# Zero-padded low halves, a fused BK and 14 earlier projection matmuls in the recurrent features of a hybrid block

## The chip, the cores and the metric

One NeuronCore of a Trainium2 chip runs the whole kernel. The metric is the device time of one execution in microseconds (us). A core has five instruction streams that run side by side and wait for one another through semaphores: TensorE (PE, with its weight loads shown apart as PEld), VectorE (DVE), ScalarE (ACT), GpSimd (POOL) and SyncE (SP, which here starts most DMAs). Each stream runs its own instructions in order.

## The reference, cut to what matters

One transformer-like layer on 1024 tokens of width 1024: a wide input projection, dilated window attention on part of it, an RWKV-7 recurrence on another part, a gated mix of both, and a mixture of 32 experts. The change is in the features of the recurrence:

```python
pm = pf + (prev - pf) * shift_mu                  # pf: the projection p = rms_norm(x) @ w_in
r, k, v, xw, xa, xg = split(pm)
decay = exp(-exp(-softplus(-(w0 + tanh(xw) @ w_up)) - 0.5))
a  = sigmoid(a0 + xa @ a_up)                      # w_up and a_up: 64 x 512, the "lora" weights
kk = normalize_per_head(k * k_k)
k  = k * (1 + (a - 1) * k_a)
o  = wkv7_scan(r, decay, k, v, kk, kk * a)        # state update by -kk and by kk*a
```

## The kernel before, in words

**Numbers.** A float32 product is made of three TensorE products: both operands are split into a high part (type F32R) and a low part, and high x high, high x low and low x high are summed in PSUM. For the lora products the contraction has only 64 rows. So the input tile `xw` holds the high part of tanh(xw) in rows 0 to 63 and its low part in rows 64 to 127 (`xa` the other way round), the host gives the weights twice, and one 128-row matmul with `lh` (L572) makes high x high and high x low. The third product, low weights by high input, is a matmul over 64 rows, `ll[hrs[n]]` by `t[hrs[n]]` (L573).

**Stages.** Up to about 110 us the kernel loads x and projects the first columns. From 110 to about 400 us it makes the recurrent features (`prep(p)`, p = 0 to 3, each with two halves h of 512 tokens; below they are half 0 to half 7 in the order of time). Then come the scan over chunks, the attention (to about 900 us), the mix, the routing, and the experts (from about 1180 us to the end).

**Fillers.** The projection of the remaining columns is cut into single 128x512 matmuls (L306), 48 for one column tile, and kept in a list of generators. `fill(n)` takes the next n of them; calls of `fill` stand all over `prep`, the scan and the attention, so that TensorE has work while the chain of small steps goes on. `fill` also steps the triangular solve (`tstep_`) once in 14 matmuls. What is left over is done by `need` before the next `prep`, or after the scan. The program order is not the final one: a scheduler orders the instructions of each engine by its own estimate of when their inputs are there, so a filler can land ahead of or behind the place at which it was written.

**One half of `prep`.** Four lora matmuls (L572, L573) make `pw` and `pa`. A small matmul (L578) and a chain of 12 tiny DVE steps give the norm of kk, ACT spreads it (L583), and PE transposes it (L588) beside the transposes of v (L592). DVE makes `kk` (L611), a running sum (L602) and, through ACT's exponentials, `P`, `iP` and `sg`. POOL makes half of `AR` (L618) from the tile `tc`, which DVE's L624 overwrites afterwards. Then come the other half of `AR` (L616) and the tile `BK`: its outer quarters from `kp` (L626), its middle from `kk * a * iP` (L628 to L630). `t2` (L632) is for a side result. PE transposes BK in 8 matmuls (L642), and multiplies BK by AR in 32 matmuls over 64 rows (L667). `split_w` turns each new weight tile of the projection into `wh` on ACT (L275) and `wl` on DVE (L277); `wh` has two buffers.

Of the kernel before, what the change touches and what calls it, by code (L numbers as in the profile page):

```python
# [10 lines left out]
F32 = mybir.dt.float32  # L11
F32R = mybir.dt.float32r
# [4 lines left out]
ALU = mybir.AluOpType  # L17
# [8 lines left out]
DEC = math.exp(-0.5)  # L26
FT, FS, FP, FA, FU, GL = 20, 6, 2, 9, 9, 10
FI, FQ, TP, FR, SQ, SG, SB, UJ, QW, QL, QT, QJ = 14, 2, 1, 16, 1, 0, 1, 1, 1, 0, 0, 1
LP, LB, LR, PF, MP, QB, GB, NY = 0, 0, 0, 1, 0, 1, 2, 2
DILS = (1, 4, 16)  # L30
NEG = -1e30
# [150 lines left out]
def block_kernel(ctx, tc, I, out, dbg=None):  # L182
    nc = tc.nc
# [96 lines left out]
    def pb(shape):  # L280
        return psB.tile([128] + shape, F32, name="pb")
# [38 lines left out]
    for k in range(8):  # L320
# [4 lines left out]
        if k == 7:  # L325
# [3 lines left out]
                                       op0=ALU.mult, op1=ALU.subtract)  # L329
        for i in range(2):  # L330
            for kk in ([k] if i == 0 or k > 1 else [] if k == 0 else [0, 1]):
                for h in range(2):
                    hs = slice(h * 512, (h + 1) * 512)
                    for n, (a, b) in enumerate(((0, xhi), (0, xlo), (1, xhi))):
                        nc.tensor.matmul(ps0[i][h], w0[i][a][:, kk, :], b[:, kk, hs],
                                         start=(kk == 0 and n == 0), stop=(kk == 7 and n == 2))
    for h in range(2):
        hs = slice(h * 512, (h + 1) * 512)
        for k in range(8):
            for n, (a, b) in enumerate(((0, xhi), (0, xlo), (1, xhi))):  # L340
                nc.tensor.matmul(ps0[2][h], w0[2][a][:, k, :], b[:, k, hs], start=(k == 0 and n == 0),
                                 stop=(k == 7 and n == 2))
# [22 lines left out]
    def tstep(n=1):  # L365
        for _ in range(n):
            if side and next(side[0], 1) == 1:
                side.pop(0)
# [21 lines left out]
    def fill(n):  # L390
        while n > 0 and fillers:
            try:
                next(fillers[0])
                n -= 1
                filled[0] += 1
                if filled[0] % FI == 0:
                    tstep()
            except StopIteration:
                fillers.pop(0)
# [11 lines left out]
    hrs = [slice(0, 64), slice(64, 128)]  # L411
# [32 lines left out]
    p1 = s1.enter_context(tc.tile_pool(name="p1a", bufs=1, reuse_waits="tile"))  # L444
# [33 lines left out]
    for p in range(4):  # L478
        cs = slice(128 * p, 128 * p + 128)
        for h in range(2):  # L480
            hs = slice(h * 512, (h + 1) * 512)
            ps = pb([512])
# [28 lines left out]
    p1 = s1.enter_context(tc.tile_pool(name="p1", bufs=1, reuse_waits="tile"))  # L511
# [2 lines left out]
    Bm = p1.tile([128, 4, 2, 2, 64], F32, name="Bm")  # L514
    nc.gpsimd.memset(Bm, 0.0)

    rkv = {}

    def rkv_steps(p):
# [24 lines left out]
    def prep(p):  # L544
# [6 lines left out]
        lr = p1.tile([128, 2, 128], F32, name="lr")  # L551
        nc.sync.dma_start(lr, I["lora"][p])
        lh = p1.tile([128, 2, 128], F32R, name="lh")
        nc.scalar.activation(lh, lr, AF.Copy)
        ll = p1.tile([128, 128], F32R, name="ll")
        for n, hr in enumerate(hrs):
            nc.vector.tensor_tensor(ll[hr], lr[hr, n], lh[hr, n].bitcast(F32), op=ALU.subtract)

        def tstep():
            if TP:  # L560
                tstep_()
            fill(FP)
        for h in range(2):
            hs = slice(h * 512, (h + 1) * 512)
            j0 = 4 * h

            def T(tag):
                return p1.tile([128, 512], F32, tag=tag, name=tag)

            pw, pa = pb([512]), pb([512])  # L570
            for n, (ps, t) in enumerate(((pw, xw), (pa, xa))):
                nc.tensor.matmul(ps, lh[:, n], t[:, hs], start=True, stop=False)  # L572
                nc.tensor.matmul(ps, ll[hrs[n]], t[hrs[n], hs], start=False, stop=True)  # L573
            kks = T("ta")
            nc.scalar.activation(kks, k[:, hs], AF.Square, scale=pc("kk", p))
            pn = pb([8])
            for j in range(4):
                nc.tensor.matmul(pn[:, 2 * j:2 * j + 2], kks[:, j * 128:(j + 1) * 128], cc("ind2"),  # L578
                                 start=True, stop=True)
# [11 lines left out]
            for j in range(4):  # L591
# [6 lines left out]
            at = T("at")  # L598
# [6 lines left out]
            iP = T("iP")  # L605
# [4 lines left out]
            kk = T("kk")  # L610
            nc.vector.scalar_tensor_tensor(kk, k[:, hs], pc("kk", p), pr.rearrange("q a b -> q (a b)"),  # L611
                                           op0=ALU.mult, op1=ALU.mult)
            AR = p1.tile([128, 4, 256], F32, name="AR")
            BK = p1.tile([128, 4, 256], F32, name="BK")
            c4 = lambda ap: ap.rearrange("q (c t) -> q c t", t=128)
# [3 lines left out]
                                    op=ALU.mult)  # L619
# [5 lines left out]
            for c in range(2):  # L625
                nc.vector.tensor_tensor(BK[:, :, 192 * c:192 * c + 64], c4(kp)[:, :, 64 * c:64 * c + 64],  # L626
                                        c4(iP)[:, :, 64 * c:64 * c + 64], op=ALU.mult)
            nc.vector.tensor_scalar(at, at, 0.5, 0.5, op0=ALU.mult, op1=ALU.add)  # L628
            nc.gpsimd.tensor_tensor(kk, kk, at, op=ALU.mult)
            nc.vector.tensor_tensor(BK[:, :, 64:192], c4(kk), c4(iP), op=ALU.mult)  # L630
            t2 = T("ta")
            nc.vector.scalar_tensor_tensor(t2, r[:, hs], pc("rk", p), kp, op0=ALU.mult, op1=ALU.mult)  # L632
            stq.dma_start(dAR[j0:j0 + 4, :, p].rearrange("j q m -> q j m"), AR)
            tstep()

            BT = p1.tile([128, 4, 2, 128], F32, name="BT")
            for jj in range(2):
# [23 lines left out]
            for hh in range(2):  # L661
                hr = hrs[hh]
# [87 lines left out]
    for p in range(4):  # L750
        prep(p)
        if p % 2 == 1:
            side.append(solve(p // 2))
# [56 lines left out]
    for j in range(8):  # L810
# [17 lines left out]
        for c in range(2):  # L828
# [4 lines left out]
            for hh in range(2):  # L833
                hr = hrs[hh]
                pX.append(pb([4, 64]))
                for p in range(4):
                    nc.tensor.matmul(pX[hh][ra, p], AR[hr, p, 64:128] if c == 0 else AR[hr, p, 128:192], Z[hr, p],
                                     start=(p == 0), stop=True, skip_group_check=True)
# [18 lines left out]
            for hh in range(2):  # L857
                hr = hrs[hh]
                for p in range(4):
                    nc.tensor.matmul(pX[hh][ro, p], AR[hr, p, 0:64] if c == 0 else AR[hr, p, 192:256], Z[hr, p],  # L860
                                     start=(p == 0), stop=False, skip_group_check=True)
# [302 lines left out]
    for n in range(8):  # L1164
        wh, wl = wrs.pop(n)
        for h in range(2):
            hs = slice(512 * h, 512 * h + 512)
            ga = gate(1, n, h)
            ps = psA.tile([128, 512], F32, name="pa")
# [31 lines left out]
    for tag in ("ohi", "olo"):  # L1201
        t = pf.tile([128, 8, 512], F32, tag=tag, name=tag + "g")
        gas += [t[:, j] for j in range(8)]
    for h in range(2):
        hs = slice(512 * h, 512 * h + 512)
        for n in range(8):
# [3 lines left out]
            ps = psA.tile([128, 512], F32, name="pa")  # L1210
# [211 lines left out]
    for i in range(8):  # L1422
# [7 lines left out]
        for c in range(2):  # L1430
            cs = slice(512 * c, 512 * c + 512)
            ps = psA.tile([128, 512], F32, name="pa")
# [267 lines left out]
```

## Time and profile before

| what | us |
|---|---|
| median of 3 runs (lowest, highest) | 1754.18 (1747.92, 1766.67) |
| the profiled execution, its own time | 1749.15 |
| its span in the trace | 1747.4 |
| PE busy | 1667.3 |
| DVE busy | 1204.8 |
| ACT busy | 871.5 |
| POOL busy | 299.8 |

"Busy" is the time in which an instruction of that engine was under way; the rest of the span is idle. Matmuls overlap one another, so the pace of PE is read from the distance between starts, not from the duration of one. "PEclk" or the clock column is the share of its full clock that TensorE was granted: 1.00 or 0.50 in this trace, or a mean of the two over a stretch. A start time such as 160.12 is us from the span's start; "[2.41 <-DVE BK L630]" behind a row says that the engine was idle for 2.41 us before it and that the write of BK at line 630 by DVE ended this.

### The profile page before, as it was taken

What the parts mean: (1) busy time and instruction counts of PE and PEld (TensorE: products, weight loads), DVE (VectorE), ACT (ScalarE), POOL (GpSimd) and SP (SyncE); (2) the same over time, 40 slices, a digit from 0 to 9 for tenths busy, and PEclk for the clock granted to TensorE, in tenths of its full rate; (3) what the DMA queues carried; (4) which work ended last, traced back from release to release, by engine and by line L of the source; (5) the groups of instructions that cost most, each with busy time, mean ns of one, the idle gap of its engine ahead of it and who ended that gap; (6) DMA issues with size and microseconds to landing.
All of it is one profiled execution on the core that took longest, in us unless ns stands there. A gap on an engine that the chain in (4) does not pass through costs nothing. (4 is left out here: it accounts for less than half of the span.)

```text
span 1747.4 us, 25870 instructions
## 1 busy us (share of the span) xinstructions
PE 1667.3 (95%) x9395; PEld 1321.3 (76%) x9396; DVE 1204.8 (69%) x2181; ACT 871.5 (50%) x1315; POOL 299.8 (17%) x321
## 2 busy tenths in 40 slices
PE   8999999999999999999998899979999999999996
PEld 6677777777777777777777677758888888888884
DVE  5647798575664444344436666589999999998985
ACT  4523434332231233343344122278888888887774
POOL 0110113123432000000000131112222221221211
PEclk9998999799999999999999899979999999999998
DMA  8323333355762111111138884479999999999993
GB/s 292 138 74 125 95 107 115 110 193 180 232 205 85 37 38 42 43 50 43 52 113 272 253 291 144 182 250 372 375 380 373 371 368 368 371 364 372 360 371 114
DMA packets 145619, 363.44 MB, mean 208 GB/s; under 512 B 17316, under 2 KB 62772, under 8 KB 145484
## 3 DMA queue, kind: packets, MB, share of 16 engines
q1 hardware_dynamic: 123108, 303.67, 48.1%
q0 software_dynamic: 15872, 50.35, 10.3%
q10 hardware_dynamic: 6504, 7.69, 1.6%
q8 instruction: 76, 1.25, 0.3%
q14 instruction: 59, 0.48, 0.1%
HBM read 307.49 MB, written 62.29 MB: 212 GB/s over the span
## 5 line engine op out<-in xcount | busy, mean ns | idle before, releaser
L1529 PE MATMUL pb<-u,xTh 128*128 128x512 f32 x1024 | 338.6, 406 | 0.5 <-ACT xTh L1524 0.5
L306 PE MATMUL pa<-xlo,wh 128*128 128x512 f32 x736 | 307.6, 418 | 0.0
L306 PE MATMUL pa<-xhi,wl 128*128 128x512 f32 x736 | 302.3, 411 | 2.2 <-DVE wl L277 2.2
L306 PE MATMUL pa<-xhi,wh 128*128 128x512 f32 x736 | 301.5, 410 | 1.5 <-DVE raw L426 1.0
L1415 DVE TENSOR_TENSOR u<-raw,u 128x1024 fp32r<-128x1024 f32 x216 | 255.0, 1219 | 18.1 <-ACT u L1414 14.6
L1414 ACT ACTIVATE u<-raw 128x1024 fp32r<-128x1024 f32 x216 | 223.7, 1056 | 31.6 <-PE pb L1529 19.7
L1529 PEld LDWEIGHTS pb<-u,xTh 128*128 128x128 f32 x1024 | 191.4, 189 | 40.5 <-ACT xTh L1524 1.4
L1529 PE MATMUL pb<-u,xTl 128*128 128x512 f32 x512 | 207.7, 406 | 0.3 <-DVE xTl L1525 0.3
L306 PEld LDWEIGHTS pa<-xlo,wh 128*128 128x128 f32 x736 | 141.2, 192 | 40.7 <-issue 11.0
L306 PEld LDWEIGHTS pa<-xhi,wl 128*128 128x128 f32 x736 | 141.6, 192 | 34.4 <-issue 3.3
L306 PEld LDWEIGHTS pa<-xhi,wh 128*128 128x128 f32 x736 | 141.4, 192 | 34.4 <-issue 2.9
L1415 DVE TENSOR_TENSOR u<-mix,u 128x1024 fp32r<-128x1024 f32 x128 | 151.5, 1218 | 11.2 <-ACT u L1414 9.1
L1529 PE MATMUL pa<-u,hTh 128*128 128x512 f32 x512 | 143.4, 401 | 0.9 <-ACT hTh L1524 0.9
L1414 ACT ACTIVATE u<-mix 128x1024 fp32r<-128x1024 f32 x128 | 133.2, 1057 | 16.6 <-PE pb L1529 9.2
L977 DVE SCALAR_TENSOR_TENSOR Sb<-pb,rqk,bias 128x128 f32<-128x128 f32 (+1 forms) x96 | 35.5, 407 | 124.5 <-PE pb L976 116.6
L1508 POOL DMA_INDIRECT out<-row,tba x30 | 78.5, 2617 | 202.5 <-ACT u L1414 171.9
L1529 PEld LDWEIGHTS pb<-u,xTl 128*128 128x128 f32 x512 | 96.9, 189 | 18.5 <-DVE xTl L1525 1.0
L1529 PEld LDWEIGHTS pa<-u,hTh 128*128 128x128 f32 x512 | 93.5, 188 | 22.4 <-ACT hTh L1524 1.5
L275 ACT ACTIVATE wh<-wr 128x1024 fp32r<-128x1024 f32 x49 | 51.8, 1056 | 113.5 <-PE pa L306 95.1
L1529 PE MATMUL pa<-u,hTl 128*128 128x512 f32 x256 | 80.7, 396 | 1.2 <-DVE hTl L1525 1.2
L1502 POOL DMA_INDIRECT xin<-dH,tbl x32 | 38.5, 1203 | 250.7 <-PE pb L1523 247.5
L981 ACT ACTIVATE Sb<-Sb,ML 128x128 f32<-128x128 f32 (+1 forms) x96 | 42.3, 442 | 54.7 <-DVE ML L979 54.7
(415 smaller groups left out, 2872.8 us busy)
## 6 DMA issues: line engine op xcount, KB each, us to landing
raw<-in_w_expert_up SPq DMA_DIRECT2D x72, 512.0 KB, 11.7
raw<-in_w_expert_gate SPq DMA_DIRECT2D x71, 512.0 KB, 4.9
raw<-in_w_expert_down SPq DMA_DIRECT2D x71, 512.0 KB, 11.8
wr<-in_w_in SPq DMA_DIRECT2D x49, 512.0 KB, 3.5
mix<-in_w_expert_down SPq DMA_DIRECT2D x46, 512.0 KB, 13.5
mix<-in_w_expert_gate SPq DMA_DIRECT2D x42, 512.0 KB, 5.0
mix<-in_w_expert_up SPq DMA_DIRECT2D x40, 512.0 KB, 11.8
dGA<-gs POOLq DMA_DIRECT2D x32, 256.0 KB, 3.3
```

The lines of the kernel that those rows point to most:

```text
L275: nc.scalar.activation(wh, wr, AF.Copy)
L306: nc.tensor.matmul(ps, a[:, k, :], b[:, k, hs], start=(n == 0), stop=(n == 23))
L977: nc.vector.scalar_tensor_tensor(Sb[:, hh, 0:nk], pS[:, 0:nk], u.rn[:, 0, i, hh:hh + 1], u.bias[:, hh, 256 - nk:], op0=ALU.mult, op1=ALU.add)
L981: nc.scalar.activation(Sb[:, hh, 0:nk], Sb[:, hh, 0:nk], AF.Exp, bias=u.ML[:, i, hh:hh + 1], accum_out=u.ML[:, i, 2 + hh:3 + hh])
L1414: nc.scalar.activation(hi, raw, AF.Copy)
L1415: nc.vector.tensor_tensor(lo, raw, hi.bitcast(F32), op=ALU.subtract)
L1502: nc.gpsimd.indirect_dma_start(out=dst, out_offset=None, in_=src, in_offset=bass.IndirectOffsetOnAxis(ap=idx, axis=0), bounds_check=S - 1, ...
L1508: nc.gpsimd.indirect_dma_start(out=out, out_offset=bass.IndirectOffsetOnAxis(ap=idx, axis=0), in_=src, in_offset=None, compute_op=ALU.add)
L1529: nc.tensor.matmul(ps, x, w, start=first, stop=last)
```

## The change

Three edits in `prep`, and a constant `FB = 14`:

```diff
+    ll = p1.tile([128, 2, 128], F32R, name="ll")
+    nc.gpsimd.memset(ll.bitcast(F32), 0.0)
...
-        ll = p1.tile([128, 128], F32R, name="ll")
         for n, hr in enumerate(hrs):
-            nc.vector.tensor_tensor(ll[hr], lr[hr, n], lh[hr, n].bitcast(F32), op=ALU.subtract)
+            nc.vector.tensor_tensor(ll[hr, n], lr[hr, n], lh[hr, n].bitcast(F32), op=ALU.subtract)
...
-                nc.tensor.matmul(ps, ll[hrs[n]], t[hrs[n], hs], start=False, stop=True)
+                nc.tensor.matmul(ps, ll[:, n], t[:, hs], start=False, stop=True)
...
-            nc.vector.tensor_scalar(at, at, 0.5, 0.5, op0=ALU.mult, op1=ALU.add)
-            nc.gpsimd.tensor_tensor(kk, kk, at, op=ALU.mult)
-            nc.vector.tensor_tensor(BK[:, :, 64:192], c4(kk), c4(iP), op=ALU.mult)
+            nc.vector.scalar_tensor_tensor(kk, at, 1.0, kk, op0=ALU.add, op1=ALU.mult)
+            nc.vector.scalar_tensor_tensor(BK[:, :, 64:192], c4(kk), 0.5, c4(iP), op0=ALU.mult, op1=ALU.mult)
...
             tstep()
+            fill(FB)
 
             BT = p1.tile([128, 4, 2, 128], F32, name="BT")
```

First, the low part of the lora weights gets a tile of full height, set to zero once, of which each `prep` rewrites the same halves; its matmul runs over 128 rows, 64 of them zeros. Second, a = 0.5 * at + 0.5 is no longer made by a step of its own: kk becomes (at + 1) * kk on DVE, in place of a DVE step and a POOL multiplication, and the factor 0.5 goes into the product with `iP`. Third, `fill(14)` stands ahead of the transposes of BK, in each of the 8 halves. The number of fillers in the program (2208 matmuls of L306) stays the same.

Where the scheduler puts things shows in the order of the built programs. On TensorE, at the transposes of BK in half 1 (`ident` is the identity, `sg` and `at` hold the split t2; line numbers of the change are 1 to 3 higher than before). Before:

```order
L306 MATMUL pa<-xhi,wh 128x512
L306 MATMUL pa<-xlo,wh 128x512
L642 MATMUL pb<-ident,BK 128x128 x8
L306 MATMUL pa<-xhi,wl 128x512
L652 MATMUL pb<-sg,onr 128x512
L667 MATMUL pb<-AR,BK 128x128 x7
L653 MATMUL pb<-at,onr 128x512
L667 MATMUL pb<-AR,BK 128x128 x9
```

and of the change:

```order
L307 MATMUL pa<-xhi,wh 128x512
L307 MATMUL pa<-xlo,wh 128x512
L645 MATMUL pb<-ident,BK 128x128 x8
L655 MATMUL pb<-sg,onr 128x512
L656 MATMUL pb<-at,onr 128x512
L670 MATMUL pb<-AR,BK 128x128 x16
```

The fillers that stood behind the transposes have moved ahead of them, but not 14 at each place. Counted over all halves, the fillers between the transposes of kk's norm and v (L588, L592) and those of BK were 27, 28, 35, 35, 31, 32, 36, 25, and are 28, 31, 36, 28, 27, 38, 37, 28 (half 5 has matmuls of the solve in between). Ahead of L588 they were 21, 13, 17, 13, 43, 37, 15, 16 (counted from the small matmuls L578) and are 21, 15, 17, 21, 36, 38, 12, 20.

On VectorE, the stretch from `kk` to BK in half 1, before:

```order
L611 SCALAR_TENSOR_TENSOR kk<-k,pv,pb 128x512
L622 TENSOR_SCALAR ta<-at,ka_377 128x512
L628 TENSOR_SCALAR at<-at 128x512
L600 TENSOR_SCALAR sg<-sg 128x512
L602 SCALAR_TENSOR_TENSOR tb<-cv,sg 128x512
L607 TENSOR_TENSOR sg<-tb,sg 128x512
L624 TENSOR_TENSOR tc<-k,ta 128x512
L616 TENSOR_TENSOR AR<-sg,kk 128x4x128
L626 TENSOR_TENSOR BK<-tc,iP 128x4x64 x2
L630 TENSOR_TENSOR BK<-kk,iP 128x4x128
L632 SCALAR_TENSOR_TENSOR ta<-r,pv,tc 128x512
```

and of the change:

```order
L614 SCALAR_TENSOR_TENSOR kk<-k,pv,pb 128x512
L603 TENSOR_SCALAR sg<-sg 128x512
L625 TENSOR_SCALAR ta<-at,ka_377 128x512
L605 SCALAR_TENSOR_TENSOR tb<-cv,sg 128x512
L610 TENSOR_TENSOR sg<-tb,sg 128x512
L627 TENSOR_TENSOR tc<-k,ta 128x512
L619 TENSOR_TENSOR AR<-sg,kk 128x4x128
L629 TENSOR_TENSOR BK<-tc,iP 128x4x64 x2
L631 SCALAR_TENSOR_TENSOR kk<-at,kk 128x512
L634 SCALAR_TENSOR_TENSOR ta<-r,pv,tc 128x512
L632 SCALAR_TENSOR_TENSOR BK<-kk,iP 128x4x128
```

The step on `at` (L628) is gone and the running sum stands one place earlier; the new product kk (L631) stands behind the outer quarters of BK, and t2 has come ahead of the last step of BK, which is now the last of the three.

Also on VectorE, the end of the norm's chain in half 3 (`rn`, `rsq_z`: the norm's tiny tiles; `wl`: the low part of the next weight tile). Before:

```order
L262 TENSOR_TENSOR rsq_z<-rn 128x8
L263 TENSOR_TENSOR rsq_z<-rsq_z,rsq_u 128x8
L264 SCALAR_TENSOR_TENSOR rn<-rsq_z,rn 128x8
L534 TENSOR_TENSOR raw<-pa,rstdB 128x512
L611 SCALAR_TENSOR_TENSOR kk<-k,pv,pb 128x512
```

and of the change:

```order
L263 TENSOR_TENSOR rsq_z<-rn 128x8
L538 TENSOR_TENSOR raw<-pa,rstdB 128x512
L264 TENSOR_TENSOR rsq_z<-rsq_z,rsq_u 128x8
L278 TENSOR_TENSOR wl<-wr,wh 128x1024
L265 SCALAR_TENSOR_TENSOR rn<-rsq_z,rn 128x8
L540 SCALAR_TENSOR_TENSOR v<-raw,pv,v 128x512
L603 TENSOR_SCALAR sg<-sg 128x512
L614 SCALAR_TENSOR_TENSOR kk<-k,pv,pb 128x512
```

Here `wl`, and what it waits for, has come ahead of the norm's last step; half 7 has the same.

More of the change, by code (lines that the diff above doesn't have):

```diff
@@ L28 @@
 FI, FQ, TP, FR, SQ, SG, SB, UJ, QW, QL, QT, QJ = 14, 2, 1, 16, 1, 0, 1, 1, 1, 0, 0, 1
+FB = 14
 LP, LB, LR, PF, MP, QB, GB, NY = 0, 0, 0, 1, 0, 1, 2, 2
```

## The prediction

> **What bounds the kernel now.** I read the page's busy times first, then the busy time by stage, then TensorE's waits and its clock inside the stage of the change.
>
> ```profile
> PE 1667.3 (95%) x9395; PEld 1321.3 (76%) x9396; DVE 1204.8 (69%) x2181; ACT 871.5 (50%) x1315; POOL 299.8 (17%) x321
> ```
>
> TensorE is under way for 95% of the span. The rows by stage (from:to, length, then busy PE, PEld, DVE, ACT and POOL with counts, the granted clock, DMA share, GB/s) say where the other 5% is:
>
> ```profile
> 110.00:400.00 290.00, 270.09 (x1536) 213.88 (x1535) 222.83 (x522) 108.47 (x190) 51.63 (x76) 0.91 0.38 125
> 400.00:640.00 240.00, 234.85 (x2281) 184.39 (x2279) 124.74 (x314) 66.21 (x127) 63.06 (x86) 1.00 0.40 127
> 640.00:900.00 260.00, 259.24 (x1439) 189.89 (x1439) 105.96 (x224) 100.40 (x251) 12.85 (x21) 1.00 0.17 58
> ```
>
> The stage of the change is the first row. It has 20 us without a matmul and a mean clock of 0.91. The next two stages are filled by TensorE (235 of 240, 259 of 260), so what the first stage saves is handed on. The experts read their weights through DMA, but not before the mix has given its buffers back:
>
> ```profile
> 1080.00:1120.00 40.00, 39.94 (x210) 31.63 (x209) 23.43 (x118) 10.81 (x28) 8.06 (x8) 1.00 0.31 111
> 1180.00:1737.00 557.00, 551.66 (x2564) 458.21 (x2562) 513.83 (x515) 452.65 (x512) 115.09 (x60) 1.00 0.99 357
> ```
>
> DMA is at 0.31 shortly before and at 0.99 from 1180 us on. So the weight stream is not already running full when the experts begin; it starts from a point that compute sets and moves with it. The chain that ended last is of no use here: it holds only the last 1.7 us.
>
> TensorE's idle time in the first stage is mostly one wait, for BK; these are its six places in the order of time:
>
> ```profile
> PE pb L642 <- DVE BK L630: 13.2, 6, 2.6
> 160.12 1.48 PE L642 MATMUL pb<-ident,BK 128*128 128x128 f32 x8 [2.41 <-DVE BK L630]
> 195.18 1.06 PE L642 MATMUL pb<-ident,BK 128*128 128x128 f32 x8 [2.20 <-DVE BK L630]
> 223.07 1.06 PE L642 MATMUL pb<-ident,BK 128*128 128x128 f32 x8 [2.62 <-DVE BK L630]
> 255.52 1.06 PE L642 MATMUL pb<-ident,BK 128*128 128x128 f32 x8 [0.76 <-DVE BK L630]
> 326.82 1.06 PE L642 MATMUL pb<-ident,BK 128*128 128x128 f32 x8 [2.63 <-DVE BK L630]
> 361.94 1.89 PE L642 MATMUL pb<-ident,BK 128*128 128x128 f32 x8 [2.57 <-DVE BK L630]
> ```
>
> These are halves 1, 2, 3, 4, 6 and 7. The second loss stands right behind some of them (stretch, length, busy PE, clock, DMA share, GB/s):
>
> ```profile
> 160.60:174.30 13.70, 13.70 (x52) 0.50 0.30 96
> 193.00:198.00 5.00, 2.82 (x16) 1.00 0.49 161
> 220.40:227.00 6.60, 3.98 (x27) 1.00 0.34 120
> 327.90:351.80 23.90, 23.90 (x83) 0.50 0.22 77
> 362.00:365.40 3.40, 3.40 (x13) 0.50 0.00 1
> ```
>
> After the gaps of 2.41, 2.63 and 2.57 us TensorE works at half clock for 13.7, 23.9 and 3.4 us; after those of 2.20 and 2.62 us it keeps the full clock. So a gap of this size may cost the clock or not. What half clock means is the distance between fillers:
>
> ```profile
> 121.37 0.63 PE L306 MATMUL pa<-xhi,wh 128*128 128x512 f32 x1
> 121.80 0.63 PE L306 MATMUL pa<-xlo,wh 128*128 128x512 f32 x1
> 123.32 0.39 PE L306 MATMUL pa<-xhi,wl 128*128 128x512 f32 x1
> 123.55 0.40 PE L306 MATMUL pa<-xhi,wh 128*128 128x512 f32 x1
> ```
>
> 0.43 us against 0.23 (0.235 over longer runs): 45% of a half-clock stretch is lost. The three stretches together are 41.0 us, so they cost 18.4 us.
>
> **The change part by part. Low halves.** One half's four lora matmuls and the two fillers behind them, and below them the first two fillers behind the float32 transposes:
>
> ```profile
> 141.88 0.47 PE L572 MATMUL pb<-xw,lh 128*128 128x512 f32 x1
> 142.28 0.50 PE L573 MATMUL pb<-xw,ll 64*128 64x512 f32 x1
> 142.72 0.50 PE L572 MATMUL pb<-xa,lh 128*128 128x512 f32 x1
> 143.15 0.50 PE L573 MATMUL pb<-xa,ll 64*128 64x512 f32 x1
> 143.58 0.50 PE L306 MATMUL pa<-xhi,wl 128*128 128x512 f32 x1
> 143.91 0.40 PE L306 MATMUL pa<-xhi,wh 128*128 128x512 f32 x1
> 150.91 0.47 PE L306 MATMUL pa<-xlo,wh 128*128 128x512 f32 x1
> 151.22 0.40 PE L306 MATMUL pa<-xhi,wl 128*128 128x512 f32 x1
> ```
>
> The five steps from 141.88 to 143.91 take 2.03 us, at full clock. With all of them over 128 rows I expect the fillers' 0.235, except for the first, which still follows matmuls of another type and takes 0.31 as at 150.91: 0.31 + 4 x 0.235 = 1.25. That saves 0.78 a half, **6.2 us** in 8 halves, on TensorE itself. Bounds: nothing, if it is something else than the height that slows them, and 6.9 us if the first goes at 0.235 too. I take 6.2, since it is the alternation of heights that sets these rows apart from all other 128x512 rows. [...]
>
> The zeroing of `ll` is one POOL instruction for the whole stage; POOL is busy for 51.6 of 290 us there and nothing else waits behind it for long: nothing.
>
> **BK.** Half 1 on DVE and POOL:
>
> ```profile
> 150.86 0.75 DVE L611 SCALAR_TENSOR_TENSOR kk<-k,pv,pb 128x512 f32<-128x512 f32 x1 [0.80 <-PE pb L588]
> 152.90 1.22 DVE L602 TENSOR_TENSOR_SCAN tb<-cv,sg 128x512 f32<-128x512 f32 x1
> 156.34 0.69 DVE L624 TENSOR_TENSOR tc<-k,ta 128x512 f32<-128x512 f32 x1 [1.49 <-POOL AR L618]
> 157.55 1.82 DVE L626 TENSOR_TENSOR BK<-tc,iP 128x256 f32<-128x256 f32 x2
> 159.29 0.68 DVE L630 TENSOR_TENSOR BK<-kk,iP 128x512 f32<-128x512 f32 x1
> 159.90 0.74 DVE L632 SCALAR_TENSOR_TENSOR ta<-r,pv,tc 128x512 f32<-128x512 f32 x1
> 157.71 1.37 POOL L629 TENSOR_TENSOR kk<-kk,at 128x512 f32<-128x512 f32 x1 [1.41 <-DVE AR L616]
> ```
>
> POOL's product hides behind L626, and L626 pays for it: two steps of 256 columns take 1.74 us to the next start while POOL runs (I take 0.66 without it, somewhat over half of the 0.61 from L630's start to the next for each). So not 0.4 + 1.4 us go, but the step on `at` (0.33) ahead of the running sum, which also moves ahead of L622: the sum starts 1.46 instead of 2.04 us after `kk`, 0.58 earlier. POOL's L618, which waits for the sum, and L624 go with it: L624 starts at 155.76. From there 0.61 (L624), 0.61 (L616), 0.66 (L626 twice), 0.67 (new kk), 0.67 (t2, now ahead), 0.74 (new BK), and 0.15 to TensorE, which is what lies between the end at 159.97 and 160.12: BK's transposes can start at 159.87 instead of 160.12. Only 0.25 us, since t2 stands in between and the fused steps are each a little longer than what they replace. The 3 fillers more that stand ahead of the transposes fill 0.70. The gap goes from 2.41 to about **1.45 us**.
>
> The same working for the others, by the same row durations and the row orders of the change; a fused step counts 0.67, a step on `at` 0.33, and a step that POOL stretched to 1.7 us (`k`'s mixing step in half 2, t2 in halves 4 and 6, the two L626 in half 7) loses about 1.0. Half 2: `at` and the stretched step of 1.7 go from ahead of BK, two fused steps and 0.06 come, 0.65 earlier in all; one filler more: 2.20 to 1.3. Half 3: four small steps ahead of the running sum (1.8) and the stretching go, the fused steps come, 2.8 us earlier from `kk` to BK; but 7 fillers fewer (1.65; they went ahead of L588): 2.62 to 1.4, and 0.5 more at L588 (below). Half 4: 1.6 earlier, 4 fillers fewer: 0.76 to 0.1. Half 6: `at` and 1.0 go, one fused step comes, 0.65 earlier; one filler more: 2.63 to 1.8. Half 7: the sum 0.8 earlier and 1.0 less stretching, two fused steps more, 0.4 earlier; 3 fillers more: 2.57 to 1.5. Sum 8.0 instead of 13.2: **5.2 us** saved. Bounds: 0 and 13.2.
>
> **14 fillers.** They add no work; what they cost is what is missing later. The stages that lose them are the ones with 235 of 240 and 259 of 260 us busy, and the projection runs on into the attention, so it is taken from a place where TensorE had work anyway: nothing. The solve steps that `fill` calls come a little earlier; DVE carries them either way.
>
> **Clock.** Of the 18.4 us I count halves 1 and 7 (6.2 and 1.5 us) as won, since their gaps shrink to 1.5 us, and half of the 10.7 us of half 6, whose 1.8 us is uncertain: **13.0 us**. Bounds: nothing and 18.4. The smallest gap that lost the clock at once is 2.41, the largest that kept it 2.62; the half clock at 121 us above stands behind none of these gaps, so a smaller one is not safe. [...]
>
> **Sum.** 6.2 + 5.2 + 13.0 = 24.4 us, from the profiled execution's own 1749.15 to 1724.8. That execution was 5.0 us faster than the median of the three runs shown (1754.18), as is plausible where the clock falls by chance; I carry this along and forecast a median of **1730 us**.
>
> **The rivals.** *The clock stays out.* The gaps shrink, but the half-clock stretches stay or come back elsewhere, because work with few active rows (L667's 64) holds the clock down once it is down: in the stretch from 327.9 on TensorE had work all the time and stayed at 0.50 for 23.9 us. Then 6.2 + 5.2 = 11 us: 1743. For it: two of the gaps kept the clock as they were, so it is not the gap's length alone. Against it: each of the three stretches starts within 1.1 us of the end of a gap.
>
> *The chain rules.* If the stage is held by the chain through DVE (222.8 of 290 us busy) and not by TensorE, then what TensorE saves in the lora matmuls becomes more waiting for BK, and since t2 now stands ahead, BK is not earlier: nothing is won, 1754. This is also what happens if the scheduler's order undoes the 14 fillers; in halves 3 and 4 it has put fewer ahead of BK than before. Against it: the chain starts at L588, and 12 or more fillers stand ahead of that in each half, so it follows TensorE's pace.
>
> *Slower: `wl` ahead of the norm.* In halves 3 and 7 DVE must now do `wl` (L277) before the last step of the norm, and `wl` waits for ACT's `wh`, which waits for TensorE to finish a column tile:
>
> ```profile
> 209.58 0.63 ACT L583 ACTIVATE ta<-rn 128x512 f32<-128x512 f32 x1 [0.19 <-DVE rn L264]
> 210.72 1.06 ACT L275 ACTIVATE wh<-wr 128x1024 fp32r<-128x1024 f32 x1 [0.51 <-PE pa L306]
> 215.56 1.20 DVE L277 TENSOR_TENSOR wl<-wr,wh 128x1024 fp32r<-128x1024 f32 x1
> ```
>
> From the tile's last filler to L588 go 1.06 for L275, 1.20 for L277, 0.2 for the norm's tiny step, 0.63 for L583 and some 0.5 for hand-overs of 0.15 each, 3.6 us; TensorE has 13 fillers, 3.1 us. That is the 0.5 us above. If ACT has something else before it, or POOL stretches `wl` as it does L626, the gap passes 2.4 us from 2 us of delay on, and TensorE loses its clock there. Two new gaps of 2.5 us, each with a stretch like the longest one (10.7 us), are 26 us, against 11 won: 15 us slower, 1769.
>
> **How the numbers follow.** Forecast 0.47 (1715 to 1737, the low end from the upper bounds 6.9, 9 of the gaps, and 18.4), clock stays out 0.28 (1737 to 1748), chain rules 0.15 (1748 to 1760), slower 0.10. The range takes the first two and part of the third: 1716 to 1752. Faster by over 1% (below 1736.6) is the forecast and a little of the second: 0.50; within 1%: 0.40; slower: 0.10. One per cent is about what a measurement of this kernel can tell from no change; its three runs spread over 1.1%.
>
> **What would show it.** Low halves: the four lora matmuls start 0.24 us apart at full clock. BK: POOL's product is gone, two L626 steps take under 0.9 us, t2 lies directly ahead of the last BK step, and TensorE's wait at BK is near 8 us in six places instead of 13.2. Clock: over 0.95 in the stage, with no stretch at 0.50 over 10 us. The stage ends some 24 us earlier, and the later ones are as long as before. I am wrong if the gaps grow, if a wait at L588 appears, or if the clock is below 0.91 there.

## The result and the profile after

The changed kernel takes **1726.52 us** (median of 4 runs, 1724.14 to 1729.95) against 1756.53 for the kernel before beside it: ratio 0.9843, 95% interval 0.9806 to 0.988. Run once more later, it took 1727.87 us (median of 5; ratio 0.9882, 0.9837 to 0.9927). The forecast was 1730, with a range of 1716 to 1752. The profiled execution took 1724.65 us; the sum worked out from rows was 1724.8.

The page of the changed kernel, and two rows by stage (columns as before: stretch, length, busy PE, PEld, DVE, ACT, POOL, clock, DMA share, GB/s):

```profile
span 1722.9 us, 25856 instructions
PE 1646.6 (96%) x9395; PEld 1307.5 (76%) x9396; DVE 1193.8 (69%) x2181; ACT 870.6 (51%) x1315; POOL 290.7 (17%) x314
...
110.00:400.00 290.00, 273.34 (x1959) 220.60 (x1957) 228.33 (x551) 117.14 (x205) 52.90 (x86) 0.98 0.41 138
1155.00:1712.00 557.00, 552.40 (x2570) 458.85 (x2568) 513.99 (x515) 453.29 (x514) 115.18 (x60) 1.00 0.99 357
```

In the same 290 us TensorE got through 1959 matmuls instead of 1536, at a clock of 0.98 instead of 0.91, while its busy time hardly moved (273 against 270 us). Of the 423 more, 352 are small ones of the solve and the scan, which have moved into the window. The clock, more than the busy share, shows the gain. The experts' stage is the row of before moved by 25 us: 552 us busy in 557, DMA at 0.99.

In the list of TensorE's waits (us in total, times, longest) the one for BK, and below it from the timeline the six gaps ahead of BK's transposes and one at the solve:

```profile
PE pb L645 <- DVE BK L632: 7.6, 6, 1.6
```

```profile
161.45 1.06 PE L645 MATMUL pb<-ident,BK 128*128 128x128 f32 x8 [1.37 <-DVE BK L632]
188.35 1.06 PE L645 MATMUL pb<-ident,BK 128*128 128x128 f32 x8 [1.57 <-DVE BK L632]
213.52 1.06 PE L645 MATMUL pb<-ident,BK 128*128 128x128 f32 x8 [1.46 <-DVE BK L632]
240.12 1.06 PE L645 MATMUL pb<-ident,BK 128*128 128x128 f32 x8 [0.19 <-DVE BK L632]
311.30 1.06 PE L645 MATMUL pb<-ident,BK 128*128 128x128 f32 x8 [1.51 <-DVE BK L632]
335.84 1.06 PE L645 MATMUL pb<-ident,BK 128*128 128x128 f32 x8 [1.47 <-DVE BK L632]
380.46 1.20 PE L730 MATMUL pb<-YT,LW 32*32 32x32 f32 x64 [1.64 <-DVE YT L722]
```

7.6 us instead of 13.2. The row at 335.84 stands 26.1 us earlier than its counterpart at 361.94. Behind these gaps the clock holds; what is left of half clock lies ahead of half 1 and behind the solve's wait (rows by stretch):

```profile
119.20:126.00 6.80, 6.80 (x19) 5.54 (x20) 5.23 (x17) 2.76 (x6) 1.47 (x2) 0.50 0.31 96
126.00:382.00 256.00, 241.52 (x1594) 195.58 (x1594) 216.43 (x522) 104.65 (x185) 42.80 (x68) 1.00 0.43 144
382.00:385.40 3.40, 3.40 (x79) 2.55 (x79) 0.00 (x0) 0.87 (x2) 3.23 (x6) 0.50 0.51 154
```

A second profile, of the later execution at 1727.87 us, has the same 7.6 us of gaps at BK and no half clock behind them either. It has half clock at 119.2 and 382.0 us as well, but also in two places more, behind waits of 1.20 us for the next `wl` and of 1.38 us at the solve in half 5:

```profile
259.20:262.60 3.40, 3.40 (x8) 2.72 (x9) 3.40 (x12) 1.41 (x2) 0.00 (x0) 0.50 0.53 159
279.60:286.40 6.80, 6.80 (x141) 5.92 (x141) 2.88 (x4) 5.70 (x11) 3.52 (x7) 0.50 0.37 113
```

In the first profile waits of 1.20 and 1.56 us stand at these two places, and the clock held. So what a gap there does to the clock differs from one execution to the next.

From the timeline of the first profile the lora matmuls of half 1 with two fillers, and DVE's steps around the fused ones:

```profile
143.47 0.48 PE L575 MATMUL pb<-xw,lh 128*128 128x512 f32 x1
143.78 0.39 PE L576 MATMUL pb<-xw,ll 128*128 128x512 f32 x1
144.01 0.40 PE L575 MATMUL pb<-xa,lh 128*128 128x512 f32 x1
144.25 0.39 PE L576 MATMUL pb<-xa,ll 128*128 128x512 f32 x1
144.48 0.40 PE L307 MATMUL pa<-xhi,wl 128*128 128x512 f32 x1
144.72 0.40 PE L307 MATMUL pa<-xhi,wh 128*128 128x512 f32 x1
```

```profile
158.68 0.76 DVE L629 TENSOR_TENSOR BK<-tc,iP 128x256 f32<-128x256 f32 x2
159.35 0.69 DVE L631 SCALAR_TENSOR_TENSOR kk<-at,kk 128x512 f32<-128x512 f32 x1
159.95 0.75 DVE L634 SCALAR_TENSOR_TENSOR ta<-r,pv,tc 128x512 f32<-128x512 f32 x1
160.61 0.69 DVE L632 SCALAR_TENSOR_TENSOR BK<-kk,iP 128x512 f32<-128x512 f32 x1
```

Five steps from 143.47 to 144.72 are 1.25 us instead of 2.03; seven of the eight halves have 1.24 to 1.31, and half 0, which holds a wait for `ll`, has 1.63. Where the 0.2 us of each step went shows in the weight loads (PEld) of the first low half, before and after:

```profile
142.28 0.18 PEld L573 LDWEIGHTS pb<-xw,ll 64*128 64x128 f32 x1 [0.24 <-issue]
143.55 0.19 PEld L576 LDWEIGHTS pb<-xw,ll 128*128 128x128 f32 x1
```

Over 64 rows the load starts at 142.28, together with its own matmul; at full height it starts 0.23 us ahead of its matmul at 143.78, beside the matmul in front. The two L629 take 0.67 to the next start instead of 1.74, t2 (L634) stands ahead of BK's last step, and TensorE starts 0.15 us after that.

### The profile page after: what moved, and what is told of

It is laid out like the page before. It is cut to its first block, busy times and chain, and to the rows that moved or that the text cites. A ratio compares the mean times of both kernels' runs of the same rounds, so it can differ in the third digit from the quotient of the medians.

```text
span 1722.9 us, 25856 instructions
## 1 busy us (share of the span) xinstructions
PE 1646.6 (96%) x9395; PEld 1307.5 (76%) x9396; DVE 1193.8 (69%) x2181; ACT 870.6 (51%) x1315; POOL 290.7 (17%) x314
## 3 DMA queue, kind: packets, MB, share of 16 engines
q8 instruction: 76, 1.25, 0.3%
## 5 line engine op out<-in xcount | busy, mean ns | idle before, releaser
L307 PE MATMUL pa<-xhi,wl 128*128 128x512 f32 x736 | 297.9, 405 | 2.3 <-DVE wl L278 2.3
L1417 ACT ACTIVATE u<-raw 128x1024 fp32r<-128x1024 f32 x216 | 223.6, 1056 | 31.6 <-PE pb L1532 18.4
## 6 DMA issues: line engine op xcount, KB each, us to landing
mix<-in_w_expert_down SPq DMA_DIRECT2D x46, 512.0 KB, 13.2
```

The lines of the kernel that those rows point to most:

```text
L307: nc.tensor.matmul(ps, a[:, k, :], b[:, k, hs], start=(n == 0), stop=(n == 23))
L1417: nc.scalar.activation(hi, raw, AF.Copy)
```

## The experiments

Times are compared with the kernel before run beside each, by ratio with its interval, since that kernel's own median went from 1751.8 to 1757.5 us from one set of runs to the next. Lines are those of each kernel.

**One edit at a time.** *Low halves alone* (the diff's first edit on the kernel before):

> The kernel before with the low halves in full-height tiles alone; the order on TensorE is that of before. Theory (each term stands by itself: pace of the lora matmuls, gaps at BK, clock): the five steps from the first lora matmul take 1.25 us instead of 2.03, 6 us are saved on TensorE, the gaps at BK stay near 13 us and their half-clock stretches stay, so the time is 3 to 9 us under that of before and the clock of the stage about 0.91. Rival (the chain through DVE holds the stage): the pace improves as well, but the gaps grow by the same 6 us to about 19, and the time does not move.

Measured 1739.97 us, ratio 0.9905 (0.9871 to 0.9939). Its wait for BK, and its row by stage:

```profile
PE pb L644 <- DVE BK L632: 13.2, 6, 2.6
```

```profile
110.00:400.00 290.00, 269.53 (x1575) 217.38 (x1574) 229.29 (x542) 109.00 (x191) 52.35 (x78) 0.93 0.39 129
```

The pace is the expected one (145.20 to 146.44 us in its trace, 1.24 us), and the gaps at BK stayed at 13.2 us, so the rival, in which the gaps grow by what the pace saves, fell: DVE's chain moves with TensorE. But the time fell by 11 to 23 us (the interval on 1753.55), more than the 3 to 9 expected. Where the rest comes from is taken up below.

*Fused steps alone*:

> The kernel before with the two fused DVE steps for BK alone. The scheduler puts 28, 31, 36, 28 fillers ahead of BK's transposes in halves 0 to 3, as in the changed kernel, without any fill of 14. Theory: the fused steps close the gaps, directly and through the scheduler; gaps at BK near 8 us, none over 2 us, clock of the stage 0.97 or more, 15 to 20 us under before. Rival (the 14 fillers close the gaps): the gaps stay above 11 us, the clock near 0.91, and the time moves by less than 6 us.

Measured 1733.03 us, ratio 0.9878 (0.9813 to 0.9943). The wait for BK and the row by stage:

```profile
PE pb L641 <- DVE BK L629: 7.4, 5, 1.6
```

```profile
110.00:400.00 290.00, 272.80 (x1806) 216.68 (x1804) 227.72 (x547) 114.71 (x199) 49.15 (x77) 0.96 0.40 134
```

Gaps as in the changed kernel, without any fill of 14. The clock is a little under the 0.97 expected: a stretch of 6.8 us begins 0.7 us behind a wait for `Bm` (1.23 us) and holds one for the next weight tile (1.59), and one of 17 us begins at the end of the window, behind the solve.

*14 fillers alone*:

```diff
             tstep()
+            fill(14)
 
             BT = p1.tile([128, 4, 2, 128], F32, name="BT")
```

> The kernel before with fill(14) ahead of the transposes of BK alone. In halves 0 to 3 the order on TensorE is exactly that of before. Theory: gaps of halves 1 to 3 as before (2.2 to 2.6 us), the others within 1 us, clock between 0.88 and 0.94, time within 8 us of before, either way. Rival (the fillers close the gaps): gaps under 9 us and 15 us or more saved.

Measured 1755.42 us, ratio 0.9999 (0.9956 to 1.0042): nothing. Its longest waits of TensorE between 100 and 420 us:

```profile
PE pb L643 <- DVE BK L630: 12.8, 6, 2.6
PE pb L728 <- DVE YT L720: 5.6, 2, 4.1
```

The gaps of halves 1, 2, 3 and 7 are those of before. In half 4 the gap is 1.35 instead of 0.76 us, in half 6 1.68 instead of 2.63, and at the solve (YT) a wait of 4.1 us appears. That the fillers used up early are what is missing there is the likely reason; no run shows it apart.

**One edit undone.** *The changed kernel without the 14 fillers*:

> The changed kernel without the 14 fillers. In halves 0 to 3 the order is that of the changed kernel; from half 4 on it differs. Theory (the fused steps move the fillers, and the fill of 14 is worth nothing): gaps at BK 7 to 8 us, time within 4 us of the changed kernel, 1723 to 1731. Rival (what the fill of 14 takes from later stages costs something, or what it adds helps): over 5 us away, with waits in halves 4 to 7 or in the solve that differ by as much.

Measured 1726.45 us, ratio 0.9827 (0.9773 to 0.9882): the same as with them. From both sides, then, the third edit is worth nothing that can be measured. The gaps at BK are 7.4 us, and no half clock follows them; but this one profile, of an execution at 1732.16 us, has 10.2 and 20.5 us at half clock in half 5, the first from within a wait of 1.60 us for `Bm`, the second behind one of 1.34 us at the solve.

*The changed kernel with 64-row low halves*:

> The changed kernel with the low halves put back to 64 rows; every instruction stands in the order of the changed kernel. Theory (pace alone): the five steps from the first lora matmul take 2.03 us again, the gaps at BK stay at 7 to 8 us, the clock of the stage stays at 0.97 or more, and the time is 5 to 8 us above the changed kernel, 1731 to 1735, ratio to before about 0.988. Rival (the 64-row matmuls also count less for the clock, which would explain why the low halves alone gained 13 us): more half-clock stretches, clock of the stage under 0.96, 12 us or more above the changed kernel, ratio 0.991 or more.

Measured 1730.17 us, ratio 0.9847 (0.98 to 0.9893); gaps 7.7 us. The median is 3.7 us above the changed kernel's, in the direction of the theory and under its 5 to 8; the intervals overlap, so by itself this run doesn't tell the size. The interval ends at 0.9893, under the 0.991 that the rival asked for.

So by the medians of their sets the fused steps alone take 20.5 us off, the low halves alone 13.6, and both together (no fill) 31.0. Beside the fused steps there are two measures of the low halves: 3.7 us with the 14 fillers, and 6.6 us without them (1733.03 with the fused steps alone, 1726.45 with both; DVE's and ACT's order is the same in these two, and TensorE's up to neighbouring 32x32 matmuls). Neither is clear of the noise. 20.5 and 13.6 are 34.1, 3 more than 31.0, which the intervals don't tell from a plain sum.

**The gap made longer, all else in the same order.** One unused POOL product where the removed one stood:

```diff
             nc.vector.tensor_tensor(AR[:, :, 64:192], c4(sg), c4(kk), op=ALU.mult)
+            dm = T("dm")
+            nc.gpsimd.tensor_tensor(c4(dm), AR[:, :, 64:192], AR[:, :, 64:192], op=ALU.mult)
```

> The changed kernel, with one POOL product of 128x512 added in each half right behind AR, its result unused, where the removed product on kk was; every other instruction stands in the same order as in the changed kernel. Theory (POOL's product stretches the DVE steps beside it, the gap grows, and a gap over 2 us can lose the clock): the two L629 steps take 1.7 us instead of 0.67, the gaps at BK rise from 7.6 to 13 us, one to four half-clock stretches come behind them, the clock of the stage falls below 0.96, and the time is 10 to 30 us above the changed kernel. Rival (the clock falls by chance, whatever the gap): gaps as said, but the clock stays at 0.98 and only the 5 to 6 us of the gaps are lost. Second rival (POOL does not slow DVE): no gap grows, no time is lost.

Measured 1742.53 us, ratio 0.9952 (0.9916 to 0.9988): 16.0 us above the changed kernel by the medians, 12 to 19 by the ratios against its two sets of runs. From its timeline POOL and DVE in half 1, then the wait for BK, and the stage and two stretches in it:

```profile
158.03 1.16 POOL L620 TENSOR_TENSOR dm<-AR 128x512 f32<-128x512 f32 x1 [1.41 <-DVE AR L618]
157.87 1.60 DVE L630 TENSOR_TENSOR BK<-tc,iP 128x256 f32<-128x256 f32 x2
159.39 0.68 DVE L632 SCALAR_TENSOR_TENSOR kk<-at,kk 128x512 f32<-128x512 f32 x1
```

```profile
PE pb L646 <- DVE BK L633: 12.6, 6, 2.4
```

```profile
110.00:400.00 290.00, 269.56 (x1785) 218.57 (x1784) 232.32 (x546) 113.86 (x199) 54.27 (x84) 0.94 0.40 132
...
161.70:165.10 3.40, 3.40 (x15) 2.75 (x14) 2.48 (x5) 2.94 (x6) 0.10 (x1) 0.50 0.08 29
318.70:328.90 10.20, 10.20 (x42) 9.04 (x42) 6.18 (x17) 3.08 (x8) 0.56 (x1) 0.50 0.29 103
```

No instruction of TensorE or DVE was added or moved. DVE's two steps (L630) took 1.52 us to the next start while POOL worked, instead of 0.67; the gaps grew by 5.0 us; and the time by about three times as much. The profile shows where the rest can go: two stretches at 0.50 follow gaps of 2.24 and 2.37 us, and at 45% they cost 6 us of an execution that was itself one of the faster ones (1737.23 us). That clock makes up the rest over all ten executions is taken up below. Two such products in each half:

> As pool_beside, with two unused POOL products in each half instead of one; the order of all else is that of the changed kernel. Theory (the clock is lost more often, the longer the gap): two more DVE steps are stretched, the gaps at BK rise from 12.6 to 16 to 20 us, most of the five long ones (3 us or more each) are followed by half clock, and the time is 1755 to 1775. Rival (the clock falls by chance): the gaps' own 4 to 7 us above pool_beside (1742.5), so under 1750.

Measured 1758.65 us, ratio 1.0048 (1.0022 to 1.0074): slower than the kernel before, and 30.8 us above the changed kernel beside it. The wait for BK, the stage, and four stretches in it:

```profile
PE pb L647 <- DVE BK L634: 17.7, 6, 3.3
```

```profile
110.00:400.00 290.00, 265.16 (x1523) 216.54 (x1522) 223.40 (x512) 107.20 (x188) 57.71 (x83) 0.89 0.36 118
166.10:176.30 10.20, 10.20 (x42) 8.87 (x41) 8.68 (x21) 3.46 (x9) 0.10 (x1) 0.50 0.39 129
224.10:237.80 13.70, 12.64 (x51) 11.21 (x52) 9.64 (x23) 4.84 (x10) 0.68 (x2) 0.50 0.17 59
336.80:347.00 10.20, 10.20 (x43) 8.95 (x42) 6.22 (x18) 3.63 (x9) 0.56 (x1) 0.50 0.28 103
367.50:377.70 10.20, 10.20 (x44) 8.92 (x43) 6.24 (x18) 2.98 (x8) 0.56 (x1) 0.50 0.28 103
```

Gaps of 3.1 to 3.3 us now lose the clock in four places of five. Gap total 7.6, 12.6, 17.7 us; time 1726.5 to 1727.9, 1742.5, 1758.7 us; clock of the stage 0.98, 0.94, 0.89 (one profile of each). Had the clock fallen by chance, whatever the gap, the gaps' own 5.0 and 10.1 us would have given 1732 and 1737, by estimate.

**Low halves where the gaps are long.** The same POOL product once, with the low halves at 64 rows:

> pool_beside with the low halves put back to 64 rows. Theory (64-row matmuls also keep the clock down where it has been lost, so the low halves are worth more where the gaps are long): 10 us or more above pool_beside, 1752 or more. Rival (pace alone, the same everywhere): 4 to 7 us above pool_beside, 1746 to 1750.

Measured 1764.14 us, ratio 1.0051 (1.0013 to 1.0089), against 0.9952 (0.9916 to 0.9988) with full height: 1.0%, 17 us (21.6 by the medians), where the pace alone would give 4 to 7. The wait for BK, and two stretches of its trace:

```profile
PE pb L644 <- DVE BK L631: 12.1, 6, 2.4
```

```profile
193.30:203.50 10.20, 10.20 (x42) 8.86 (x41) 7.13 (x19) 3.14 (x8) 0.28 (x2) 0.50 0.23 79
224.10:248.00 23.90, 23.90 (x83) 19.53 (x82) 12.90 (x38) 7.13 (x14) 0.15 (x2) 0.50 0.26 88
```

The gaps are no longer than with full height, but half clock lasted 23.9 us here, as it did once in the kernel before; behind a gap at BK no stretch of the three full-height kernels with long gaps (low halves alone, one and two POOL products) was over 13.7. By itself that is weak: the kernel with the 14 fillers alone, which has 64 rows, has none over 13.7 there either, and the full-height one without the fillers was at half clock for 20.5 us in half 5.

One profile of each kernel is little, but the mean granted clock of its span is on record for every execution. Over the 55 executions of the kernel before that ran beside these kernels, 0.001 of this clock went with 1.5 us of time. An estimate from that, from the gaps at BK and from the pace (6.2 us for the low halves) can be set against the medians:

| slower kernel, against | mean clock (medians) | by clock, us | gaps and pace, us | sum | measured |
|---|---|---|---|---|---|
| one POOL product, changed kernel | 0.9735, 0.980 | 10 | 5.0 | 15 | 16.0 |
| two POOL products, changed kernel | 0.968, 0.980 | 18 | 10.1 | 28 | 30.8 |
| 64 rows, full height: one POOL product in both | 0.963, 0.9735 | 16 | 5.7 | 21 | 21.6 |
| 64 rows, full height: kernel before, low halves alone | 0.971, 0.9775 | 10 | 6.2 | 16 | 13.6 |
| 64 rows, full height: changed kernel | 0.982, 0.980 | -3 | 6.3 | 3 | 3.7 |
| 64 rows, full height: fused steps, no fill | 0.978, 0.9785 | 1 | 6.2 | 7 | 6.6 |

So the height is worth its pace, 4 to 7 us, where the gaps are short, and 14 to 22 us where they are long, and there the rest is clock by this estimate (10 and 16 us). How 64 rows take the clock is open. In the profiles, gaps of 2.2 to 2.6 us at BK lost it in 8 of 14 places with 64 rows and in 4 of 10 with full height, which is too few to tell whether it is lost more often, or for longer.

**Further on.** Three kernels tried to take away what is left.

```diff
-            kp = T("tc")
+            kp = T("kp")
```

> The changed kernel with the tile kp in a buffer of its own, so that DVE's product kp no longer waits for POOL to have read the tile tc. The fillers ahead of BK's transposes are then 18, 27, 39, 42, 27, 38, 39, 30. Theory (the rest of the gaps comes from DVE's wait of 1.5 us for POOL's half of AR): the gaps at BK fall from 7.6 to 2 to 5 us, 3 to 6 us are saved against the changed kernel, 1720 to 1724. Rival (POOL's half of AR now runs beside more DVE steps and stretches them, so that as much comes back): gaps at 6 us or more, time within 2 us of the changed kernel.

Measured 1724.15 us, ratio 0.9827 (0.9772 to 0.9883); gaps 5.5 us in all. A part of theory and rival each: L624's wait for POOL is gone and the gaps shrink by 2.1 us, but in halves 1, 3 and 6 one of BK's outer quarters now takes 1.25 to 1.48 us to the next start instead of 0.34, beside POOL's half of AR.

```diff
-        nc.sync.dma_start(lr, I["lora"][p])
+        (nc.scalar if p == 0 else nc.sync).dma_start(lr, I["lora"][p])
```

> The changed kernel with the first lora weights loaded through ACT's queue instead of SP's; the scheduler then puts their high part (lh) ahead of the mixing steps of k on ACT, and the later order changes with it: 28, 42, 18, 31, 19, 34, 28, 30 fillers ahead of BK's transposes. Theory (the wait of 1.85 us for lh ahead of half 0 costs itself and the half-clock stretch of 6.8 us behind it): no wait for lh over 0.5 us, no half clock between 115 and 126 us, 4 to 5 us saved, unless the gaps at BK grow where fewer fillers stand ahead (half 2 and half 4: up to 3 us each), which would lose as much again. Rival (the clock falls there whatever the wait): the stretch stays, under 2 us saved.

Measured 1725.92 us, ratio 0.9838 (0.9782 to 0.9894). The wait for `lh` is gone and so is the half clock at 119 us, but TensorE waits 2.97 us for `wh` instead, and loses its clock for 3.4 us there. Both edits together, with the longest waits of TensorE between 100 and 420 us:

> kp in a buffer of its own and the first lora weights through ACT's queue, both on the changed kernel. Fillers ahead of BK's transposes 18, 42, 18, 31, 20, 34, 30, 30. Theory (both waits go): gaps at BK under 5 us in all, 3 to 8 us under the changed kernel beside it. Rival (the scheduler's new order puts as much waiting elsewhere, as the 2.97 us for wh in lh_early): within 2 us of the changed kernel.

```profile
PE pa L306 <- ACT wh L275: 3.0, 1, 3.0
PE pb L729 <- DVE YT L721: 2.9, 2, 1.7
PE pb L590 <- ACT ta L585: 2.8, 3, 1.1
PE pb L644 <- DVE BK L631: 2.1, 3, 0.8
```

Measured 1726.90 us beside 1727.87 of the changed kernel: the rival. The gaps at BK are 2.1 us, and the waits for `wh` and for the norm (L590) have taken their place. None of the three is distinguishable from the changed kernel.

## Why the prediction was right, point by point

- **What bounds.** Right: the end moved by 24.5 us (span 1747.4 to 1722.9), after 26.1 us at the last BK. The stages behind handed it on.
- **Low halves, 6.2 us.** The pace was met (1.25 us a half). At full clock a step at which the height changes took 0.40 to 0.44 us (the four from 141.88 to 143.58), and one at which it doesn't 0.23 to 0.24 (the four from 143.78 to 144.72). The weight load over 64 rows that starts only with its own matmul (142.28) goes with the longer steps; why it starts so late, no run shows. What the forecast lacked is that the height also matters to the clock where gaps are long: alone it was worth 13.6 us, of which 6.2 are pace, and with one POOL product in both kernels the mean clock was 0.9735 with full height and 0.963 with 64 rows. The term came out nevertheless, since the fused steps had made the gaps short.
- **BK, 13.2 to 8.0 us.** The 8.0 were some 7.5 of gaps and 0.5 at L588. The gaps measured 7.6: 1.37, 1.57, 1.46, 0.19, 1.51, 1.47 against 1.45, 1.3, 1.4, 0.1, 1.8, 1.5. The working behind them holds too: from the start of `kk` to the end of BK it is 0.33, 0.39, 2.87, 1.91, 0.87 and 0.49 us less than before, where it had 0.25, 0.65, 2.8, 1.6, 0.65 and 0.4. The 0.5 us at L588 in half 3 did not come; one of 1.07 us came at its counterpart in half 5, and the second profile of the changed kernel has none over 0.15 us in the stage.
- **14 fillers, nothing.** Right, and more literally than the text had it: the 3 fillers more in half 1 that it sets against the gap are there without the third edit. So it is the fused steps that made the scheduler move them; by what estimate isn't shown.
- **Clock, 13.0 of 18.4 us.** Right in direction, too small in size. In the first profile all three stretches are gone, and so is one of 6.8 us at 273.3 that the working did not count; 6.8 us at 119.2 (3.4 before) and 3.4 us at 382.0 are left. From 110 to 400 us that is 10.2 us at half clock instead of 51.2, which at 45% is 18 us; the second profile has 17.1, which is 15. That the clock is lost with longer gaps at BK is now shown by the two POOL kernels (0.94 and 0.89 in the stage). That the length alone decides is not: near 2.4 us the clock is lost only sometimes (in 12 of 24 places with 2.2 to 2.6 us), and at the solve gaps of 1.3 to 1.7 us sometimes lose it too.
- **The sum, 24.4 us.** The 24.5 us between the two profiled executions, 1724.65 us against 1724.8, are partly luck. By the rows the three terms are about 6, 5.6 and 18 us, some 5 more than 24.5. Other waits took back 1.8 of it, since TensorE's idle time in the whole span fell by 3.8 us (80.1 to 76.3) where the gaps at BK fell by 5.6; the rest is not traced to a row. The 5.0 us carried from the profiled execution to the median were 1.9 in the changed kernel.
- **The rivals.** *The clock stays out* and *the chain rules* fell with the stage's clock of 0.98 and with the low halves alone, whose gaps did not grow. A little of the first is in the second profile, where 10.2 us of half clock came back in half 5. That work with few active rows holds the clock down, as that rival had it, was the author's guess and isn't shown: with the low halves at 64 rows too, the mean clock was lower in one pair (0.963 against 0.9735, one POOL product) and not in another (0.982 against 0.980, the changed kernel). *Slower* did not occur: `wl` ahead of the norm cost no wait in half 3 or half 7.

## What to carry to other kernels

Where TensorE is the bound, look at its granted clock beside each gap before adding up gaps: here 5 us more of gaps cost 16 us, and 10 us more cost 31. Where the clock varies from one execution to the next, compare its mean over all of them (0.976 to 0.984 in five executions of the changed kernel), since one profile shows one draw. A helper's product on POOL that seems free costs what DVE loses beside it (here 0.85 us, 1.52 instead of 0.67 for two steps), and DVE's delay can be what TensorE waits for (12.6 instead of 7.6 us at BK). Keep small products at the height of their neighbours (here 0.235 instead of 0.43 us a step), and count in the built order, not in the source, what a call for fillers moved.

## What the runs showed of the hardware that was not expected

- At BK, half clock followed gaps of 2.2 to 2.6 us in 12 of 24 places (five kernels), gaps of 3.1 to 3.3 us in four of five, and gaps of 1.3 to 1.7 us in none of 32. Around the solve gaps of 1.2 to 1.7 us were enough at times, among them 1.20, 1.38 and 1.70 us in the second profile of the changed one. Half clock came in lengths near multiples of the shortest, 3.4 us (6.8, 10.2, 13.7, 17.1, 20.5, 23.9); no run shows why.
- Once lost, the clock stayed at 0.50 for up to 23.9 us with TensorE busy throughout; both stretches of that length hold the 32 matmuls over 64 rows of L667 and 20 or 21 fillers.
- Two DVE steps of 128x256 float32 with two inputs take 0.67 us alone and 1.52 to 1.74 us beside one POOL product of 128x512.
